# The cached pages of a decode step as a four-stage pipeline in a ring of 1 MB units

## The chip, the cores and the metric

The kernel runs on one core of a Trainium2 chip. The metric is device time in microseconds (us) of one execution, as the median of three runs. Engines are named as in the profile: PE is TensorE (matmuls; PEld its weight loads), DVE is VectorE, ACT is ScalarE, POOL is GpSimd, SP is SyncE, which here mostly issues DMAs. A name with a q (SPq) is an engine's sequencer.

## The reference, cut to what matters

The program is one step of a two-layer hybrid decoder, in float32, for a prompt of 1024 tokens and for 8 samples of 4 new tokens each. A layer has a combined input projection, a gated delta rule recurrence (4 heads) beside differential attention (8 key heads of 64, 4 value heads of 128), an output projection, cross attention and a gated MLP. For the samples, differential attention also looks at 4096 past tokens, which lie in pages of 128 tokens and are found through a table:

```python
past_k = cache_k[l][page_table].reshape(Bs, past_len, 2 * DIFF_H, DIFF_DH)
past_v = cache_v[l][page_table].reshape(Bs, past_len, DIFF_H, DIFF_DV)
...
s = jnp.einsum('bqhd,bkhd->bhqk', qi, k).astype(jnp.float32) * scale
p = jax.nn.softmax(s, axis=-1).reshape(B, H, 2, qb, Lk)
a = p[:, :, 0] - lam * p[:, :, 1]
return jnp.einsum('bhqk,bkhe->bqhe', a.astype(v.dtype), v)
```

Per layer and sample these are 32 key pages and 32 value pages of 256 KB, so 128 MB of keys and values in each of the two layers.

## The kernel before, in words

The program is written as generators that record instructions and yield a cost. `interleave` always continues the generator that has used the least of its budget. In each layer two run together: the main stream (`rest`: projections, recurrence, attention of the prompt; then `post`: output projection, cross attention, MLP for the first half of the tokens) with a budget of 520 + 2 x 450, and the page stream (`dec`, then `dec_end`) with 152. The second half of `post` follows alone. A scheduler then sets the order of each engine's queue from the recorded order, from priorities, and from its own model of when operands are ready; on the chip every engine works through its queue in that order and waits where an operand is not there. `prio(n)` moves what is recorded in it ahead by n places in the scheduler's eyes.

`dec` goes through the samples one after the other. For keys it has 8 steps S per sample, each of four pages. A half step loads two pages into a tile `kn` (`pages`, ring of 3 of 512 KB) and transposes them on DVE into half of a tile `T` (L653). When both are there, 16 matmuls (L657, in `prio(20000)`) give scores in the PSUM tile `sc`, which after four steps are reduced to a maximum and copied to `p` (two buffers). After step 7 comes the exponential on ACT, then 8 transposes of `p` on PE (L672, also in `prio`) with copies to `pT`. Then 8 steps of values: four pages are loaded into `vn`, and four matmuls (L681, in `prio`) add to the PSUM tile `po`. `T` and `vn` share one ring of four buffers of 1 MB, tag `pg`. So a key load is recorded right ahead of its transpose, and a value load right ahead of its matmuls.

`pages` reads the page numbers into SP's registers and issues one DMA of 256 KB for each page on SP. It keeps the page loads in their order, and behind the weight fetch recorded last (`anchor`; `issue_after` sets an order in a queue and no wait). The weights are fetched on SP too (`fetch`, L315), into a ring `raw`; ACT casts a tile to `whi` (L332) and POOL makes the rest `wlo` (L333); three matmuls a product use them (L353 to L355). SP takes fetches and page loads from one queue, in order.

Of the kernel before, what the change touches and what calls it, by code (L numbers as in the profile page):

```python
# [9 lines left out]
F32 = mybir.dt.float32  # L10
# [9 lines left out]
P = 128  # L20
# [3 lines left out]
NB = 8  # L24
# [159 lines left out]
def build(tc, a, out, depth=2):  # L184
# [20 lines left out]
    v_, s_, g_, t_ = nc.vector, nc.scalar, nc.gpsimd, nc.tensor  # L205
# [380 lines left out]
    for l in range(depth):  # L586
# [38 lines left out]
        def dec_open():  # L625
# [5 lines left out]
            qs = dk.tile([P, 2048], F32, name="qs", tag="pg", bufs=4)[0:32, 0:512]  # L631

        def dec():
            mlq = dk.tile([P, 16, 32], BF16, name="mlq")
# [5 lines left out]
            yield 0.1  # L640
            for b in range(NB):
                lq = dk.tile([P, 16, 32], F32, name="lq", tag="lq", bufs=1)
                g_.tensor_tensor(lq.rearrange("p a (m q) -> p a m q", q=4), bcast(Q0[:, :, 4 * b:4 * b + 4], 2, 8), mlq.rearrange("p a (m q) -> p a m q", q=4), op=ALU.mult)
                p = dk.tile([P, 1024], F32, name="p", tag="p", bufs=2)
                m2 = dk.tile([P, 2], F32, name="m2", tag="m2", bufs=2)
                for S in range(8):
                    if S % 4 == 0:
                        sc = psB((P, 512))
                    T = dk.tile([P, 4, 16, 32], F32, name="T", tag="pg", bufs=4)
                    for hf in range(2):  # L650
                        kn = dk.tile([P, 2, 512], F32, name="kn", tag="kn", bufs=3)
                        pages(b * NPG + S * 4 + 2 * hf, 2, lambda i: kn[:, i, :], lambda r: ckl[bass.ds(r, 1)].rearrange("o t h d -> (o t) (h d)"))
                        v_.transpose(T[:, 2 * hf:2 * hf + 2].rearrange("p s j b -> p (s j b)"), kn.rearrange("p s d -> p (s d)"))  # L653
                    with prio(int(XP[3])):
                      for j in range(4):
                        for c in range(4):
                            t_.matmul(sc[32 * c:32 * c + 32, (S % 4) * P:(S % 4 + 1) * P], lq[:, 4 * c + j, :], T[:, :, 4 * c + j, :], start=(j == 0), stop=(j == 3))  # L657
                    if S % 4 == 3:
                        v_.tensor_reduce(m2[:, S // 4:S // 4 + 1], sc, axis=AX.X, op=ALU.max)
                        evac(p[:, (S // 4) * 512:(S // 4) * 512 + 512], sc)  # L660
                    yield 1.2
# [1439 lines left out]
```

## Time and profile before

| What | Value |
|---|---|
| median of three runs | 4379.74 us (4379.24 to 4381.07) |
| the profiled execution | 4376.1 us, its span 4374.0 us |
| PE, PEld busy | 3896.6 us (89%), 3308.6 us (76%) |
| DVE, ACT, POOL busy | 2542.2, 1483.0, 1580.3 us |
| mean granted PE clock | 0.943 |
| bytes read from and written to HBM | 589.71 MB, 79.25 MB |

The span is the time from the first to the last instruction in the trace; the execution's own time is 2.1 us more. Busy time counts an engine's work without its waits. The granted clock is the share of TensorE's full 2.4 GHz that the chip granted; at each moment it is 1.0 or 0.5. Idle time of an engine that is not the bottleneck costs nothing.

### The profile page before, as it was taken

The numbers are of one execution on the slowest core, as the hardware profiler recorded it, in microseconds if no ns is written. First come the engines' busy times: TensorE is split into PE (matmuls) and PEld (weight loads), VectorE is DVE, ScalarE is ACT, GpSimd is POOL, SyncE is SP. The second block draws the span as 40 slices with busy tenths as digits, with TensorE's granted clock in tenths as the row PEclk, the third lists the DMA queues.
The fourth block names the chain that finished last, engine by engine and source line by source line (L and its number), as shares of the span: only waits on it lengthen the run. The fifth ranks groups of instructions, "written<-read, shape, count | busy, mean of one in ns | idle before, by whom it ended". The sixth has DMA issues, their size and how long they took to land. (4 is left out here: it accounts for less than half of the span.)

```text
span 4374.0 us, 77980 instructions
## 1 busy us (share of the span) xinstructions
PE 3896.6 (89%) x28558; PEld 3308.6 (76%) x28558; DVE 2542.2 (58%) x4573; ACT 1483.0 (34%) x3086; POOL 1580.3 (36%) x1402
## 2 busy tenths in 40 slices
PE   6999988888888998899989998888789899989999
PEld 5888856676666678899989886666666666878999
DVE  7536747655555654566576275667366555456555
ACT  4333443433222224333233253334242222342222
POOL 6542422132333343444446142311323233424442
PEclk8999979998999999999999998899889999999999
DMA  5657677567687764322246467654758876532222
GB/s 171 180 142 185 190 178 205 127 199 192 165 206 189 203 162 126 98 74 83 84 118 192 122 186 203 195 146 126 205 155 217 215 200 160 158 97 74 84 84 75
DMA packets 684806, 674.11 MB, mean 154 GB/s; under 512 B 70397, under 2 KB 501448, under 8 KB 684424
## 3 DMA queue, kind: packets, MB, share of 16 engines
q1 hardware_dynamic: 637909, 638.99, 53.7%
q10 hardware_dynamic: 44851, 25.81, 1.9%
q8 instruction: 226, 3.70, 0.4%
q0 software_dynamic: 1664, 4.33, 0.3%
q14 instruction: 156, 1.28, 0.1%
HBM read 589.71 MB, written 79.25 MB: 153 GB/s over the span
## 5 line engine op out<-in xcount | busy, mean ns | idle before, releaser
L333 POOL TENSOR_TENSOR wlo<-raw,whi 128x1024 fp32r<-128x1024 f32 (+1 forms) x472 | 929.5, 1977 | 1291.6 <-ACT whi L332 1228.9
L353 PE MATMUL psA<-ph,whi 128*128 128x272 f32 (+2 forms) x2784 | 884.7, 320 | 37.3 <-ACT ph L389 17.7
L354 PE MATMUL psA<-pl,whi 128*128 128x272 f32 (+2 forms) x2784 | 882.5, 318 | 12.4 <-POOL pl L392 12.4
L355 PE MATMUL psA<-ph,wlo 128*128 128x272 f32 (+2 forms) x2784 | 881.4, 318 | 0.0
L332 ACT CAST whi<-raw 128x1024 fp32r<-128x1024 f32 (+1 forms) x472 | 407.4, 873 | 1027.6 <-PE psA L354 565.4
L353 PEld LDWEIGHTS psA<-ph,whi 128*128 128x128 f32 x2784 | 533.8, 193 | 89.5 <-ACT ph L389 21.1
L354 PEld LDWEIGHTS psA<-pl,whi 128*128 128x128 f32 x2784 | 535.7, 193 | 53.8 <-POOL pl L392 14.2
L355 PEld LDWEIGHTS psA<-ph,wlo 128*128 128x128 f32 x2784 | 534.4, 192 | 41.0 <-issue 11.6
L653 DVE STREAM_TRANSPOSE T<-kn 128x1024 f32<-128x1024 f32 x256 | 315.8, 1237 | 181.1 <-DMA kn<-in_cache_k_dram 170.9
L353 PE MATMUL psA<-ah,whi 128*128 128x272 f32 (+2 forms) x948 | 313.0, 346 | 24.8 <-DVE fcv L2006 14.8
L2020 DVE TENSOR_TENSOR x<-x,psA 128x272 f32<-128x272 f32 (+2 forms) x474 | 233.8, 516 | 167.7 <-PE psA L355 164.3
L354 PE MATMUL psA<-al,whi 128*128 128x272 f32 (+2 forms) x948 | 307.5, 337 | 7.9 <-DVE al L309 7.7
L355 PE MATMUL psA<-ah,wlo 128*128 128x272 f32 (+2 forms) x948 | 295.1, 335 | 9.9 <-POOL wlo L333 9.9
L353 PE MATMUL psA<-hi,hh 128*128 128x256 f32 (+3 forms) x864 | 252.8, 294 | 36.0 <-DVE cxn L744 28.7
L681 PE MATMUL psC<-vn,pT 128*32 128x512 f32 x1024 | 154.4, 680 | 133.3 <-DMA vn<-in_cache_v_dram 117.2
L353 PE MATMUL psA<-hh,whi 128*128 128x352 f32 x768 | 255.4, 333 | 5.5 <-ACT whi L332 5.5
L355 PE MATMUL psA<-hi,hl 128*128 128x256 f32 (+3 forms) x864 | 251.0, 291 | 6.1 <-POOL hl L392 3.5
L355 PE MATMUL psA<-hh,wlo 128*128 128x352 f32 x768 | 253.7, 331 | 1.0 <-POOL wlo L333 1.0
L354 PE MATMUL psA<-hl,whi 128*128 128x352 f32 x768 | 254.4, 331 | 0.0
L354 PE MATMUL psA<-lo,hh 128*128 128x256 f32 (+3 forms) x864 | 251.5, 292 | 0.0
L353 PEld LDWEIGHTS psA<-ah,whi 128*128 128x128 f32 x948 | 184.0, 197 | 76.1 <-DVE fcv L2006 21.2
L309 DVE TENSOR_TENSOR al<-fcv,ah 128x272 fp32r<-128x272 f32 (+2 forms) x134 | 200.8, 1502 | 63.9 <-ACT ah L308 63.4
(553 smaller groups left out, 7970.3 us busy)
## 6 DMA issues: line engine op xcount, KB each, us to landing
kn<-in_cache_k_dram SPq DMA_DIRECT2D x512, 256.0 KB
vn<-in_cache_v_dram SPq DMA_DIRECT2D x512, 256.0 KB
raw<-in_w_gate_dram SPq DMA_DIRECT2D x88, 512.0 KB
raw<-in_w_up_dram SPq DMA_DIRECT2D x88, 512.0 KB
raw<-in_w_down_dram SPq DMA_DIRECT2D x88, 512.0 KB
qksc<-ctt ACTq DMA_DIRECT2D x128, 128.0 KB
raw<-in_w_in_dram SPq DMA_DIRECT2D x128, 128.0 KB
raw<-in_w_out_dram SPq DMA_DIRECT2D x32, 512.0 KB
```

Source lines behind the costliest of these rows:

```text
L309: eng.tensor_tensor(lo, src, hi.bitcast(F32), op=ALU.subtract)
L332: s_.copy(hi, raw)
L333: g_.tensor_tensor(lo, raw, hi.bitcast(F32), op=ALU.subtract)
L353: t_.matmul(ps, ahi, bhi, start=(i == 0), stop=False)
L354: t_.matmul(ps, ahi, blo, start=False, stop=False)
L355: t_.matmul(ps, alo, bhi, start=False, stop=(i == n - 1))
L653: v_.transpose(T[:, 2 * hf:2 * hf + 2].rearrange("p s j b -> p (s j b)"), kn.rearrange("p s d -> p (s d)"))
L681: t_.matmul(po[32 * i:32 * i + 32, :], pT[:, i, S, :], vn[:, i, :], start=(S == 0), stop=(S == 7))
L2020: v_.tensor_tensor(x[:, ot, cs], x[:, ot, cs], ps, op=ALU.add)
```

## The change

`dec` is written anew. Its work is cut into units of 1 MB: four key pages or four value pages, all in one ring of four buffers (tag `pg`), while `T` gets a ring of its own (tag `T`, two buffers, which also takes `qs` and a tile of `dec_end`). The list `seq` sets the order of the units: the keys of sample 0; then for each sample b the keys of sample b+1 and, behind them, the values of b. At the step of unit i four things are recorded: the load of unit i+3; for a key unit its transposes; the score matmuls of the key unit of the step before (`late`); for a value unit its matmuls. The transposes of the probabilities of sample b-1 are recorded after key unit 2 of sample b. `p` has one buffer.

The matmuls are no longer in `prio`. `Tracked` notes the last instruction that the main stream recorded on DVE and PE, and `behind` queues the page stream's instructions on that engine behind it. The line of every DVE and PE instruction is thereby that of the wrapper, L217. The budget is 153 for 152.

```diff
-                    T = dk.tile([P, 4, 16, 32], F32, name="T", tag="pg", bufs=4)
-                    for hf in range(2):
-                        kn = dk.tile([P, 2, 512], F32, name="kn", tag="kn", bufs=3)
-                        pages(b * NPG + S * 4 + 2 * hf, 2, lambda i: kn[:, i, :], lambda r: ckl[bass.ds(r, 1)].rearrange("o t h d -> (o t) (h d)"))
-                        v_.transpose(T[:, 2 * hf:2 * hf + 2].rearrange("p s j b -> p (s j b)"), kn.rearrange("p s d -> p (s d)"))
-                    with prio(int(XP[3])):
...
+            seq = [("k", 0, S) for S in range(8)]
             for b in range(NB):
+                if b + 1 < NB:
+                    seq += [("k", b + 1, S) for S in range(8)]
+                seq += [("v", b, S) for S in range(8)]
...
+            def load(i):
+                if i >= len(seq):
+                    return
+                kind, b, S = seq[i]
+                t = dk.tile([P, 4, 512], F32, name=kind + "n", tag="pg", bufs=4)
+                pgs[i] = t
...
+            for i, (kind, b, S) in enumerate(seq):
+                load(i + 3)
+                t = pgs.pop(i)
+                if kind == "k":
+                    T = dk.tile([P, 4, 16, 32], F32, name="T", tag="T", bufs=2)
+                    with behind(v_):
+                        for hf in range(2):
+                            v_.transpose(T[:, 2 * hf:2 * hf + 2].rearrange("p s j b -> p (s j b)"), t[:, 2 * hf:2 * hf + 2].rearrange("p s d -> p (s d)"))
+                if late is not None:
+                    yield 0.6
+                    products(*late)
+                    late = None
+                if kind == "k":
+                    late = (b, S, T)
+                    if b == 1 and S == 0:
+                        queries(1)
+                    if b and S == 2:
+                        yield 0.5
+                        pT = transposed(b - 1)
+                    yield 0.6
+                    continue
...
+                with behind(t_):
+                    for j in range(4):
+                        t_.matmul(po[32 * j:32 * j + 32, :], pT[:, j, S, :], t[:, j, :], start=(S == 0), stop=(S == 7))
+                yield 1.0
...
-        for _ in interleave((chain(rest(), scaled(post(0, HALF, False), PSC)), 520.0 + PSC * 450), (chain(ahead(dec(), TUNE[6]), ahead(dec_end(), TUNE[8])), 152.0)):
+        for _ in interleave((chain(rest(), scaled(post(0, HALF, False), PSC)), 520.0 + PSC * 450), (aside(chain(dec(), dec_end())), 153.0)):
```

**First place: values of the fifth sample of layer 0, beside the MLP's weights.** In SP's queue before, raw_15190 and raw_15196 are the fetches of one gate and one up tile; each value unit is four DMAs, of which one is shown.

```order
L315 DMA raw_15190<-in_w_gate_dram 128x8x128
L315 DMA raw_15196<-in_w_up_dram 128x8x128
...
L622 DMA vn_15241<-in_cache_v_dram 32x4x512
...
L622 DMA vn_15312<-in_cache_v_dram 32x4x512
...
L315 DMA raw_15358<-in_w_gate_dram 128x8x128
```

On PE before, whi_14804 is the up tile of the group of fetches before these, and whi_15192 the cast of raw_15190.

```order
L353 MATMUL psA_15073<-ph1_13834,whi_14804 128x512
L354 MATMUL psA_15073<-pl1_13835,whi_14804 128x512
L681 MATMUL psC_14868<-vn_15241,pT_14831 32x512 x4
L355 MATMUL psA_15073<-ph1_13834,wlo_14805 128x512
...
L353 MATMUL psA_15210<-ph0_11888,whi_15192 128x512
L681 MATMUL psC_14868<-vn_15312,pT_14831 32x512 x4
```

In SP's queue of the change, raw_15920 and raw_15926 are the fetches of a gate and an up tile.

```order
L354 DMA raw_15920<-in_w_gate_dram 128x8x128
...
L661 DMA vn_15604<-in_cache_v_dram 32x4x512
...
L354 DMA raw_15926<-in_w_up_dram 128x8x128
...
L661 DMA vn_15713<-in_cache_v_dram 32x4x512
...
L661 DMA vn_15803<-in_cache_v_dram 32x4x512
```

On PE of the change, whi_15922 is the cast of raw_15920 and whi_15928 that of raw_15926.

```order
L217 MATMUL psC_15684<-vn_15604,pT_15071 32x512 x4
L217 MATMUL psA_15940<-ph0_12048,whi_15922 128x512
...
L217 MATMUL psC_15684<-vn_15713,pT_15071 32x512 x4
L217 MATMUL psA_16017<-ph0_12048,whi_15928 128x512
...
L217 MATMUL psC_15684<-vn_15803,pT_15071 32x512 x4
```

Before, vn_15241 stood behind an up fetch on SP and was used ahead of the whole gate group that was fetched ahead of it; now vn_15713 stands behind an up fetch and is used a gate group later, right ahead of that up tile's matmuls.

**Second place: the first keys of the next sample, same layer.** On DVE before, kn_15480 holds the first half unit; the product psA_15287 is made with the up tile whose fetch is raw_15196.

```order
L653 STREAM_TRANSPOSE T_15479<-kn_15480 128x1024
L2006 TENSOR_TENSOR fcv_15209<-fcv_15209,psA_15287 128x512
L653 STREAM_TRANSPOSE T_15479<-kn_15503 128x1024
L309 TENSOR_TENSOR al_15203<-fcv_15209,ah_15202 128x512
L684 TENSOR_TENSOR om_15463<-psC_14868,c_hm_1853 128x512
```

SP's queue before goes on, behind raw_15358 of the first place, with its up tile, two down tiles, one more value unit and then these keys.

```order
L315 DMA raw_15364<-in_w_up_dram 128x8x128
L315 DMA raw_15373<-in_w_down_dram 128x1024
L315 DMA raw_15379<-in_w_down_dram 128x1024
...
L622 DMA vn_15393<-in_cache_v_dram 32x4x512
...
L622 DMA kn_15480<-in_cache_k_dram 128x512
```

On DVE of the change the same place has these rows; psA_14864 is made with the up tile whose fetch is raw_14768.

```order
L217 TENSOR_TENSOR al_14775<-fcv_14562,ah_14774 128x256
L217 SCALAR_TENSOR_TENSOR fcv_14784<-fraw_14782,pvf0_127,fcv_14784 128x512 x2
L217 STREAM_TRANSPOSE T_14861<-kn_14473 128x1024 x2
L217 STREAM_TRANSPOSE T_14931<-kn_14614 128x1024 x2
L217 TENSOR_TENSOR fcv_14784<-fcv_14784,psA_14864 128x512
```

In SP's queue of the change kn_14473 is a whole unit of four DMAs.

```order
L354 DMA raw_14762<-in_w_gate_dram 128x8x128
L354 DMA raw_14768<-in_w_up_dram 128x8x128
...
L661 DMA vn_14385<-in_cache_v_dram 32x4x512
...
L661 DMA kn_14473<-in_cache_k_dram 128x512
...
L354 DMA raw_14996<-in_w_gate_dram 128x8x128
```

The transpose stands at the same place of the MLP in both; the load that feeds it has moved up SP's queue, past four fetches and two value units.

**Third place: values of the first sample of layer 0, on PE of the change.** The eight value units of the sample are vn_4880, vn_5083, vn_5349, vn_5573, vn_5900, vn_6056, vn_6204 and vn_6350; between the second (row 2247) and the third (row 2536) stand 288 other rows.

```order
L217 MATMUL psC_5734<-vn_5349,pT_4402 32x512 x4
L217 MATMUL psG_6102<-kt_6037 128x128 x4
L217 MATMUL psC_5734<-vn_5573,pT_4402 32x512 x4
L217 MATMUL psC_5734<-vn_5900,pT_4402 32x512 x4
L217 MATMUL psC_5734<-vn_6056,pT_4402 32x512 x4
L217 MATMUL psA_6799<-c_ident_63,cst_6683 27x128
...
L217 MATMUL psA_6958<-hl0_102,whi_6746 128x352
L217 MATMUL psC_5734<-vn_6204,pT_4402 32x512 x4
```

Four units stand together here, and vn_6204, whose buffer is that of vn_5349, follows 27 rows behind it.

## Rows read from the trace of the kernel before

**Rows 1.** The page's span and its part 1, busy time by engine.

```profile
span 4374.0 us, 77980 instructions
...
PE 3896.6 (89%) x28558; PEld 3308.6 (76%) x28558; DVE 2542.2 (58%) x4573; ACT 1483.0 (34%) x3086; POOL 1580.3 (36%) x1402
```

**Rows 2.** Windows: start:end, length, busy by engine, granted clock, DMA share, GB/s.

```profile
180.00:1560.00 1380.00, 1211.61 (x8860) 961.65 (x8859) 801.96 (x1406) 460.81 (x1045) 441.43 (x441) 0.93 0.70 183
1560.00:2280.00 720.00, 662.29 (x4937) 624.47 (x4935) 442.20 (x810) 246.58 (x418) 304.54 (x226) 0.96 0.33 101
2280.00:3680.00 1400.00, 1234.79 (x9079) 989.06 (x9078) 805.57 (x1462) 475.00 (x1092) 447.51 (x456) 0.93 0.68 181
3680.00:4374.00 694.00, 648.34 (x4854) 611.29 (x4852) 384.05 (x707) 222.32 (x365) 267.55 (x187) 0.98 0.31 95
```

**Rows 3.** Groups of PE: busy us, mean ns | idle before, who ended it.

```profile
L681 PE MATMUL psC<-vn,pT 128*32 128x512 f32 x1024 | 154.4, 680 | 133.3 <-DMA vn<-in_cache_v_dram 117.2 <-issue 7.7 <-ACT pT L673 2.9
L657 PE MATMUL psB<-T,lq 128*32 128x128 f32 x4096 | 146.4, 288 | 47.8 <-DVE T L653 37.0 <-POOL lq L643 2.9 <-DVE mx L1397 2.3
...
L672 PE MATMUL psC<-c_ident,p 128*128 128x128 f32 x128 | 19.8, 278 | 4.7 <-ACT p L665 4.3 <-ACT pT L673 0.4
```

**Rows 4.** Waits of PE: us in total, times, longest us.

```profile
PE psA L353 <- DVE cxn L744: 28.7, 6, 16.7
PE psA L353 <- ACT whi L332: 22.0, 6, 7.4
...
PE psA L355 <- POOL wlo L333: 10.9, 17, 1.4
```

**Rows 5.** Group of DVE: the transposes of keys.

```profile
L653 DVE STREAM_TRANSPOSE T<-kn 128x1024 f32<-128x1024 f32 x256 | 315.8, 1237 | 181.1 <-DMA kn<-in_cache_k_dram 170.9 <-issue 9.3
```

**Rows 6.** Timeline of SP, 1140 to 1200: start, us, what, count.

```profile
1141.33 7.77 SPq L622 DMA_DIRECT2D vn<-in_cache_v_dram  x8
1150.06 0.40 SPq L315 DMA_DIRECT2D raw<-in_w_gate_dram  x1
1151.29 0.72 SPq L315 DMA_DIRECT2D raw<-in_w_up_dram  x1
1153.96 9.41 SPq L622 DMA_DIRECT2D vn<-in_cache_v_dram  x8
...
1186.07 12.04 SPq L622 DMA_DIRECT2D kn<-in_cache_k_dram  x12
```

**Rows 7.** Timeline of DVE, 1185 to 1200; in brackets idle before it.

```profile
1191.24 1.25 DVE L653 STREAM_TRANSPOSE T<-kn 128x1024 f32<-128x1024 f32 x1 [4.19 <-DMA kn<-in_cache_k_dram]
```

**Rows 8.** Timeline of PE, 1160 to 1182.

```profile
1167.95 1.93 PE L681 MATMUL psC<-vn,pT 128*32 128x512 f32 x8 [2.74 <-DMA vn<-in_cache_v_dram]
...
1172.03 0.39 PE L353 MATMUL psA<-ph,whi 128*128 128x512 f32 x1
...
1179.54 0.39 PE L353 MATMUL psA<-ph,whi 128*128 128x512 f32 x1
```

**Rows 9.** Waits of SP's queue.

```profile
SPq L315 <- POOL wlo L333: 926.8, 258, 17.7
```

**Rows 10.** Windows late in the page stream of each layer.

```profile
1200.00:1400.00 200.00, 178.86 (x1184) 129.76 (x1183) 112.35 (x117) 49.06 (x64) 63.14 (x42) 0.96 0.78 201
1400.00:1560.00 160.00, 142.06 (x856) 101.38 (x855) 78.03 (x80) 37.15 (x48) 51.44 (x33) 0.98 0.81 198
...
3400.00:3680.00 280.00, 254.05 (x1556) 182.30 (x1556) 150.30 (x155) 68.71 (x88) 92.91 (x62) 0.98 0.80 204
```

**Rows 11.** Windows of 25 us, full and half empty.

```profile
1525.00:1550.00 25.00, 21.09 (x93) 13.79 (x86) 5.22 (x8) 2.10 (x2) 4.80 (x2) 0.86 1.09 218
1350.00:1375.00 25.00, 25.00 (x221) 19.82 (x220) 14.74 (x15) 11.05 (x15) 11.76 (x8) 1.00 0.45 149
```

**Rows 12.** Line L681: shortest, median and longest ns, first and last start.

```profile
L681 PE MATMUL psC<-vn,pT x1024: 589/617/1062, 324.5 to 3676.9; 128*32 128x512 f32 x171
```

**Rows 13.** Timeline of ACT, 1140 to 1170.

```profile
1160.21 1.05 ACT L332 CAST whi<-raw 128x1024 fp32r<-128x1024 f32 x1 [21.33 <-DMA raw<-in_w_gate_dram]
```

More of the change, by code (lines that the diff above doesn't have):

```diff
@@ L204, in build, with __init__, __getattr__, call @@
     QD = {'0': nc.gpsimd, '1': nc.scalar, '2': nc.sync}[XP[0]]
-    v_, s_, g_, t_ = nc.vector, nc.scalar, nc.gpsimd, nc.tensor
+    beside = [False]
+    class Tracked:
+        def __init__(self, eng):
+            self.eng, self.last = eng, None
+        def __getattr__(self, name):
+            f = getattr(self.eng, name)
+            def call(*args, **kw):
+                r = f(*args, **kw)
+                if not beside[0]:
+                    self.last = r
+                return r
+            return call
+    v_, s_, g_, t_ = Tracked(nc.vector), nc.scalar, nc.gpsimd, Tracked(nc.tensor)
+    def behind(*engs):
+        st_ = ExitStack()
+        for e in engs:
+            st_.enter_context(tc.issue_after(e.last.ins))
+        return st_
+    def aside(g):
+        while True:
+            beside[0] = True
+            try:
+                c = next(g)
+            except StopIteration:
+                return
+            finally:
+                beside[0] = False
+            yield c
     es = ExitStack()
@@ new lines, in dec, with products @@
+            cur = {}
+            def products(b, S, T):
+                if S == 3:
+                    cur["p"] = dk.tile([P, 1024], F32, name="p", tag="p", bufs=1)
+                    cur["m2"] = dk.tile([P, 2], F32, name="m2", tag="m2", bufs=2)
+                if S % 4 == 0:
+                    cur["sc"] = psB((P, 512))
+                sc, p, m2 = cur["sc"], cur.get("p"), cur.get("m2")
+                lq = lqs[b]
+                with behind(t_):
+                    for j in range(4):
@@ L675, in dec @@
-                po = psC()
-                for S in range(8):
-                    vn = dk.tile([P, 4, 512], F32, name="vn", tag="pg", bufs=4)
-                    pages(b * NPG + S * 4, 4, lambda i: vn[32 * i:32 * i + 32, :, :], lambda r: cvl[bass.ds(r, 1)].rearrange("o (i b) h e -> (o b) i (h e)", i=4))
-                    with prio(int(XP[3])):
-                      for i in range(4):
-                        t_.matmul(po[32 * i:32 * i + 32, :], pT[:, i, S, :], vn[:, i, :], start=(S == 0), stop=(S == 7))
-                    yield 0.9
@@ L683, in dec @@
[L683 to L686 removed]
+                return pT
+            late = None
+            queries(0)
+            for i in range(3):
+                load(i)
@@ L1484, in dec_end @@
         def dec_end():
-            df = Carve(dk.tile([P, 2048], F32, name="T", tag="pg", bufs=4))
+            df = Carve(dk.tile([P, 2048], F32, name="T", tag="T", bufs=2))
             nmask = cload(df, "nmask", rows=32)
```

69 lines of the change are left out of this document (42 added, 27 removed).

## The prediction

> **What bounds the kernel now.** I read the page first [rows 1]: over a span of 4374.0 us TensorE (PE) is busy for 3896.6 us (89%), no other engine for more than 58%. So the time is PE's work, what the granted clock takes from it, and the holes in it. Then the windows, cut where the page stream (the reading of the samples' cached keys and values) starts and ends in each layer [rows 2]. The two stretches with it last 1380 and 1400 us. PE is idle there for 168.4 and 165.2 us, 333.6 in all, at a mean granted clock of 0.93; the stretches without it stand at 0.96 and 0.98. DMA is busy for 0.70 and 0.68 of a stretch with the stream and for about a third of one without.
>
> Then the groups of PE, to see which matmuls the holes stand ahead of [rows 3]: 133.3 us before the stream's value products (L681), 47.8 before its score products (L657), 4.7 before its transposes (L672). That is 185.8 us, over half of 333.6, ahead of work that itself takes 320.6 us. The same rows name the releaser: the landing of the value pages for 117.2 us, and for the scores the transposes on VectorE (DVE). DVE in turn stands for 181.1 us before these transposes, 170.9 of it on key pages [rows 5].
>
> One case of each shows why. Keys: SP, whose queue issues the loads, starts the first one at 1186.07 [rows 6], and the transpose at 1191.24 has waited 4.19 us for it [rows 7]: a half unit takes 5.2 us to land and is wanted at once. Values: vn_15241 is the first of the two units whose loads start at 1153.96 [rows 6]; PE takes it at 1167.95 after 2.74 us of nothing [rows 8]. PE works in order, so every matmul behind waits as well, those of the prompt included, whose data had long been there. The scheduler was told (offset 20000) to put the stream's matmuls as early as it believed them ready; the pages come later than it believed.
>
> **What the change does, and the sum.** It is made against the profiled execution, 4376.1 us; the median of the runs is 3.6 above that.
>
> *Work.* None is added: the same 256 transposes on DVE, the same matmuls, the same 1024 page DMAs of 256 KB. SP reads 256 instead of 384 groups of page numbers; it spends 926.8 us waiting for weight buffers to come free [rows 9], so this is worth nothing, and would be if it cost something.
>
> *Lead of the loads.* This is the whole change. In the order shown first, for the fifth sample in layer 0, vn_15713 is queued right behind the fetch raw_15926 and used right before the first matmul of that fetch's weights. In the trace the up fetch of that place, raw_15196, starts at 1151.29 [rows 6], and its first matmul runs at 1179.54 [rows 8]: some 28 us, where the load of vn_15241 had 14 and was 2.74 late. For keys (second place of the order) both kernels transpose the next sample's first unit just before DVE takes the product with one up fetch's weights. Before, that unit was queued behind three value units and four more fetches after this one; now it is queued behind a single value unit, so by the same rows some 30 us ahead. The products of a key unit also come one step later than its transposes, so PE no longer waits for DVE directly.
>
> *Waits that stay.* Twice the cover is thin. (a) In the first layer four value units are used in one clump behind a long stretch of other matmuls (third place of the order): the ring of four is full till then, the next load starts only there, its use is some 25 rows later, and it is late by about a landing: 5.2 us for half a unit [rows 6, 7]. I keep 6 us. (b) The late stretches: 1200 to 1560 and 3400 to 3680 have DMA shares of 0.78, 0.81 and 0.80 [rows 10], 510 us of full DMA in 640 us, while PE is busy for 575. Without any hole in PE the share would be 510/575 = 0.89, and slices of 25 us already stand as high as 1.09, with 0.45 between them [rows 11]. Evening them out over 3 MB of ring does not get all of it. Of the 65.0 us that PE is idle there I keep half, 32. So of 185.8 us there go 185.8 - 6 - 32 = **148** (bounds: all 185.8; or half, see the first rival).
>
> *Other work freed.* DVE no longer holds the prompt's work behind a transpose. The nearest row is PE's 28.7 us of waits for cxn, which DVE makes [rows 4]; they may have nothing to do with it, or all. I take half, **14** (0 to 28.7).
>
> *Clock.* A matmul of the value group takes 589 ns at the shortest and 1062 at the longest [rows 12], about the ratio of the two levels, 2.4 and 1.2 GHz. With fewer holes the stream's stretches should come nearer to the 0.96 to 0.98 of the others. That most of the gap of 0.03 to 0.05 stays is likely, since the attention and recurrence there make holes of their own: I take 0.02 of 2780 us = **56** (0, to 0.05 x 2780 = 139).
>
> *Given back.* The waits that aren't the stream's are 333.6 - 185.8 = 147.8 us. When PE comes sooner, it meets other engines that are not ready. In the last stretch, without pages, 45.7 of 694 us are idle, 6.6%. 6.6% of the 2562 us that would be left is 169, so **+21** (0 to 60, by the 8.0% of 1560 to 2280).
>
> *At nothing.* One buffer for p instead of two: the next sample's first scores are written to it after unit 3, and the transposes that free it stand behind unit 2; what covers that is a step of other work, of which 256 share 2780 us. If it failed, the scores would wait for a copy of one tile, 16 times. Tiles moved between rings, and a budget of 153 for 152, move no work.
>
> Sum: -148 - 14 - 56 + 21 = -197, so 4179 in a profiled execution, **4183** against the median.
>
> The Trainium skill (TensorE: Matmul & The Clock Gate, Terms) values the low clock at the throttled time times one half. A mean of 0.93 over 2780 us is 389 us at half rate, so 195 us, and the sum by it would be 4376 - 148 - 14 - 195 + 21 = 4040, if the stream had caused it all. The ratio in [rows 12] agrees with the half; the 0.96 and 0.98 of the stretches without the stream [rows 2] say that part of it would stay.
>
> **New waits.** Each load now waits for the buffer used four units before, where the rings of before held 1.5 units of keys and four of T and vn; behind it on SP wait the weight fetches. That buffer is mostly free about a step before. DVE gets its two transposes of a key unit back to back, 2 x 1.237 us [rows 5], as it did when both halves had landed.
>
> **Rivals.**
> 1. *The bandwidth is the wait.* The bursts at a share over 1 would then last as long as before, wherever the loads are queued. For it: [rows 11]. Against: the 0.45 between, and a mean of 0.70. Half of the 185.8 stays, the clock gains 0.01 (28): 4376 - 93 - 28 = 4255, against the median 4259.
> 2. *The clock follows to 0.98.* For it: the last stretch. Against: 0.96 between the layers, where no page is read. 4376 - 148 - 14 - 139 + 21 = 4096, 4100 against the median.
> 3. *Slower: weights come late behind pages.* Pages are queued further ahead, on the queue of the fetches. Its place: ScalarE's cast of a gate tile. For it: a fetch issued at 1150.06 behind eight page loads [rows 6] is cast at 1160.21, after 21.33 us of waiting [rows 13]. Against: the weights are used 12 us later, at 1172.03 [rows 8], and PE's waits for them are only 22.0 and 10.9 us in the whole span [rows 4]. It decides once the 256 units cost PE more than 197/256 = 0.77 us each; at 1 us the time is 4376 - 197 + 256 = 4435, 4439 against the median. The Trainium skill (DMA: Bandwidth & Descriptors, Queues, rings and completion order) says that each DMA engine takes a ring's descriptors in order, which is this mechanism; the 10 us from issue to cast agree.
> 4. *No change.* The holes only move to the next wait of the prompt's chain: 4380. For it: ACT, DVE and POOL run chains with PE in the attention. Against: 6.6% in the last stretch.
>
> **How the numbers follow.** My forecast 0.56, with its own range of 4140 to 4230 (the 38 us that stay gone or doubled, or the clock off by 0.01, which is 28, and a little of both); rival 1 0.20; rival 2 0.12; rival 3 0.08; rival 4 0.04. A measurement of this kernel tells about 0.2% from no change. Faster by more than that: 0.56 + 0.20 + 0.12 = 0.88; within it 0.04; slower 0.08. The range of 4095 to 4300 takes in the forecast and rivals 1 and 2 with the bounds between them; outside are rivals 3 and 4 and the far end of 2, some 0.17.
>
> **What would show it.** In the profile after: idle before the value, score and transpose matmuls together about 38 us instead of 185.8; DVE's idle before its transposes under 40 instead of 181.1; mean clock of the two stretches near 0.95; and about 90 us less in each layer. If the DMA share of the late stretches comes to 0.9 and the stream's waits stay near 90, it is rival 1; if the waits of ACT's casts for fetches reach PE as waits for whi and wlo, rival 3. The prediction is wrong if the stream's waits go and the span does not follow by about as much: then they were not what bounded it.

## The result and the profile after

The changed kernel takes **4242.23 us** (median of 4 runs, 4234.21 to 4243.3) against 4380.4 beside it: ratio 0.968 (95% interval 0.966 to 0.969), 138 us less. The forecast was 4183. The sign held, and so did the range of 4095 to 4300, but 4242 lies above the forecast's own range of 4140 to 4230. Of the 197 us that it summed, 63 did not come.

The page of the changed kernel, its first lines, as in [rows 1]:

```profile
span 4240.4 us, 77767 instructions
...
PE 3860.1 (91%) x28558; PEld 3287.4 (78%) x28558; DVE 2516.0 (59%) x4574; ACT 1486.3 (35%) x3085; POOL 1575.9 (37%) x1402
```

The span falls by 133.6 us. Of that PE's busy time gives 3896.6 - 3860.1 = 36.5 and its idle time (span less busy) 477.4 - 380.3 = 97.1.

The groups of PE and DVE that answer to [rows 3] and [rows 5]; every line is now L217, the wrapper's:

```profile
L217 PE MATMUL psB<-T,lq 128*32 128x128 f32 x4096 | 155.0, 288 | 12.6 <-DVE T L217 9.6 <-POOL lq L728 3.0
...
L217 PE MATMUL psC<-vn,pT 128*32 128x512 f32 x1024 | 139.7, 624 | 3.0 <-DMA vn<-in_cache_v_dram 3.0
...
L217 PE MATMUL psC<-c_ident,p 128*128 128x128 f32 x128 | 19.5, 275 | 0.5 <-ACT pT L738 0.5
...
L217 DVE STREAM_TRANSPOSE T<-kn 128x1024 f32<-128x1024 f32 x256 | 301.3, 1217 | 41.0 <-PE psB L217 37.1 <-DMA kn<-in_cache_k_dram 3.8 <-issue 0.2
```

The stream's waits on PE are 12.6 + 3.0 + 0.5 = 16.1 us, where they were 185.8. DVE waits 3.8 us for key pages, where it was 170.9. So idle time ahead of all other matmuls went the other way: from 477.4 - 185.8 = 291.6 to 380.3 - 16.1 = 364.2, **72.6 us more**.

The windows, cut where the stream starts and ends as in [rows 2], then three late ones as in [rows 10] (columns: length, PE, PEld, DVE, ACT, POOL busy, granted clock, DMA share, GB/s):

```profile
180.00:1510.00 1330.00, 1203.58 (x8885) 964.23 (x8885) 784.67 (x1409) 463.85 (x1048) 439.04 (x445) 0.93 0.73 190
1510.00:2200.00 690.00, 638.35 (x4802) 602.78 (x4800) 418.73 (x756) 239.13 (x390) 285.94 (x201) 0.97 0.33 99
2200.00:3560.00 1360.00, 1244.23 (x9276) 998.28 (x9278) 827.99 (x1540) 490.66 (x1126) 471.68 (x482) 0.95 0.72 190
3560.00:4240.00 680.00, 636.61 (x4775) 602.32 (x4775) 376.13 (x680) 214.98 (x356) 260.70 (x183) 0.97 0.31 95
```

```profile
1200.00:1400.00 200.00, 193.21 (x1285) 141.89 (x1287) 117.20 (x126) 52.12 (x68) 70.61 (x48) 0.98 0.87 226
1400.00:1510.00 110.00, 106.02 (x529) 72.23 (x521) 47.46 (x52) 28.67 (x37) 38.50 (x26) 0.97 0.87 194
3300.00:3560.00 260.00, 250.58 (x1479) 175.54 (x1477) 139.22 (x167) 70.85 (x91) 92.40 (x61) 0.99 0.83 201
```

By this cut some time without the stream counts as part of the second stretch. From the start of the first page load to that of the last value matmul the stretches last 1375.9 and 1409.2 us before, 1327.8 and 1321.9 after: 48 and 87 us less. Between them lie 713 us in both kernels, and behind the second 697.1 and 704.5. So the gain lies in the stretches. Their clock is 0.93 and 0.95, where it was 0.93 in both.

In the late windows PE is idle for only 20.2 of 570 us (65.0 of 640 in [rows 10]), at a DMA share (of the time of the core's 16 DMA engines) of 0.83 to 0.87. The last window reaches 24 us past the stream's end; up to there, in 3300 to 3536, the share is 0.89.

The waits of PE after (us in all, times, longest), and three of the same waits before:

```profile
PE psA L217 <- DVE cxn L217: 29.6, 8, 16.7
PE psA L217 <- DVE fcv L217: 27.0, 26, 4.0
PE psA L217 <- ACT ph L428: 25.4, 11, 8.5
PE psA L217 <- ACT whi L371: 25.0, 7, 11.2
PE psA L217 <- POOL pl L431: 18.5, 10, 2.9
...
PE psA L217 <- ACT phx L1864: 13.7, 2, 9.2
...
PE psG L217 <- DMA S<-in_state_gdn_dram: 10.5, 6, 3.9
PE psA L217 <- POOL wlo L372: 9.9, 16, 1.4
```

```profile
PE psA L353 <- ACT ph L389: 17.7, 8, 4.9
PE psA L353 <- DVE fcv L2006: 14.8, 22, 3.3
PE psG L1285 <- DMA S<-in_state_gdn_dram: 1.7, 2, 1.5
```

What was given back is spread: fcv 12 us more, phx 12, S 9, ph 8, pl 6, and many small ones. Summed by the engine that ended the wait, over all matmuls but the stream's, ACT rises from 79.6 to 120.3 us, DVE from 109.8 to 131.1, DMA from 36.1 to 43.4, POOL from 57.4 to 60.7.

How far ahead a unit is loaded can be read by counting: from the issue of the first of its DMAs on SP to the first transpose or matmul that uses it. The 38th value unit, shown in [rows 6] and [rows 8] with 14 us between, is after the change:

```profile
1188.28 1.83 SPq L661 DMA_DIRECT2D vn<-in_cache_v_dram  x4
```

```profile
1215.36 1.93 PE L217 MATMUL psC<-vn,pT 128*32 128x512 f32 x16
```

27 us ahead, with no wait. Over the 128 units of a kind the median from issue to use is 4.9 us (keys) and 9.5 (values) before, 35.4 and 27.6 after.

### The profile page after: what moved, and what is told of

Read it like the earlier page. It is cut to its first block, busy times and chain, and to the rows that moved or that the text cites. A ratio compares the mean times of both kernels' runs of the same rounds, so it can differ in the third digit from the quotient of the medians.

```text
span 4240.4 us, 77767 instructions
## 1 busy us (share of the span) xinstructions
PE 3860.1 (91%) x28558; PEld 3287.4 (78%) x28558; DVE 2516.0 (59%) x4574; ACT 1486.3 (35%) x3085; POOL 1575.9 (37%) x1402
## 5 line engine op out<-in xcount | busy, mean ns | idle before, releaser
L217 PE MATMUL psA<-ph,whi 128*128 128x272 f32 (+2 forms) x2784 | 887.6, 321 | 50.4 <-ACT ph L428 25.4
L217 PE MATMUL psA<-pl,whi 128*128 128x272 f32 (+2 forms) x2784 | 880.4, 317 | 22.8 <-POOL pl L431 18.5
L217 PE MATMUL psA<-ph,wlo 128*128 128x272 f32 (+2 forms) x2784 | 877.7, 316 | 0.1
L217 PEld LDWEIGHTS psA<-ph,whi 128*128 128x128 f32 x2784 | 532.7, 192 | 126.4 <-ACT ph L428 29.3
L217 PEld LDWEIGHTS psA<-pl,whi 128*128 128x128 f32 x2784 | 535.1, 192 | 56.7 <-POOL pl L431 21.1
L217 PEld LDWEIGHTS psA<-ph,wlo 128*128 128x128 f32 x2784 | 533.9, 192 | 31.1 <-issue 1.9
L217 DVE TENSOR_TENSOR x<-x,psA 128x272 f32<-128x272 f32 (+2 forms) x590 | 285.0, 499 | 337.3 <-PE psA L217 302.9
L217 PE MATMUL psA<-ah,whi 128*128 128x272 f32 (+2 forms) x948 | 312.9, 346 | 40.8 <-DVE fcv L217 27.0
L217 DVE STREAM_TRANSPOSE T<-kn 128x1024 f32<-128x1024 f32 x256 | 301.3, 1217 | 41.0 <-PE psB L217 37.1
L217 PE MATMUL psA<-al,whi 128*128 128x272 f32 (+2 forms) x948 | 311.7, 337 | 11.4 <-DVE al L217 11.2
L217 PE MATMUL psA<-ah,wlo 128*128 128x272 f32 (+2 forms) x948 | 302.9, 335 | 9.3 <-POOL wlo L372 9.3
L217 PE MATMUL psA<-hi,hh 128*128 128x256 f32 (+3 forms) x864 | 254.6, 296 | 45.2 <-DVE cxn L217 29.6
L217 PE MATMUL psA<-hh,whi 128*128 128x352 f32 x768 | 254.0, 331 | 4.2 <-ACT whi L371 4.2
L217 PE MATMUL psA<-hi,hl 128*128 128x256 f32 (+3 forms) x864 | 249.7, 290 | 5.8 <-POOL hl L431 3.5
L217 PE MATMUL psA<-hh,wlo 128*128 128x352 f32 x768 | 253.0, 330 | 0.6 <-POOL wlo L372 0.6
L217 PEld LDWEIGHTS psA<-ah,whi 128*128 128x128 f32 x948 | 183.9, 197 | 87.7 <-DVE fcv L217 35.1
L217 PE MATMUL psA<-hl,whi 128*128 128x352 f32 x768 | 251.7, 328 | 0.0
L217 PE MATMUL psA<-lo,hh 128*128 128x256 f32 (+3 forms) x864 | 249.8, 290 | 0.1
L217 DVE TENSOR_TENSOR al<-fcv,ah 128x272 fp32r<-128x272 f32 (+2 forms) x134 | 192.1, 1437 | 76.4 <-ACT ah L347 75.8
L217 DVE TENSOR_SCALAR fcv<-fraw,pvf 128x512 f32<-128x512 f32 x88 | 126.4, 1436 | 143.3 <-ACT fraw L2080 143.2
```

Of the source, the lines that this page charges most:

```text
L217: r = f(*args, **kw)
```

## The experiments

All in one table. The ratio is to the kernel before, run on the same chip, with its 95% interval. The kernels ran in four groups, beside which the kernel before took 4380.4, 4378.57, 4368.3 and 4374.94 us, so two variants are compared by their ratios. "Issue to use" is the median just described, for keys and for values. PE's busy and idle time, the idle time ahead of the stream's matmuls, and DVE's ahead of the page transposes are those of the profiled execution, in us, which lies up to 15 us from the median of its kernel. "Behind" means queued by `behind`, after the main stream's last instruction on that engine.

| Kernel | Ratio | Issue to use | PE busy | PE idle | stream | DVE idle |
|---|---|---|---|---|---|---|
| before | 1 | 4.9, 9.5 | 3896.6 | 477.4 | 185.8 | 181.1 |
| before, matmuls behind | 0.994 (0.993 to 0.996) | 5.1, 18.8 | 3912.3 | 439.1 | 13.1 | 222.0 |
| before, transposes behind | 0.987 (0.986 to 0.989) | 14.0, 11.8 | 3867.7 | 450.4 | 153.6 | 41.8 |
| before, both behind | 0.975 (0.971 to 0.979) | 14.0, 17.9 | 3866.8 | 392.0 | 60.3 | 45.4 |
| **changed** | 0.968 (0.966 to 0.969) | 35.4, 27.6 | 3860.1 | 380.3 | 16.1 | 41.0 |
| changed, no lead | 0.970 (0.968 to 0.971) | 24.1, 20.4 | 3869.4 | 378.7 | 49.6 | 43.3 |
| changed, lead of 1 | 0.971 (0.970 to 0.973) | 29.1, 24.4 | 3863.8 | 385.8 | 29.7 | 40.8 |
| changed, matmuls with priority | 0.993 (0.991 to 0.994) | 43.7, 10.1 | 3882.2 | 478.8 | 194.7 | 2.4 |
| changed, transposes free | 0.975 (0.971 to 0.979) | 34.3, 29.5 | 3888.1 | 382.5 | 9.9 | 170.5 |
| changed, old order of units | 0.980 (0.977 to 0.984) | 30.8, 34.5 | 3885.5 | 397.9 | 34.2 | 8.0 |
| changed, scores not late | 0.974 (0.972 to 0.976) | 37.1, 26.0 | 3879.3 | 384.1 | 20.6 | 22.9 |
| changed, three T | 0.966 (0.964 to 0.967) | 26.1, 19.3 | 3874.0 | 366.9 | 30.9 | 25.6 |
| changed, budget 170 | 0.978 (0.976 to 0.980) | 32.6, 25.6 | 3877.1 | 398.9 | 15.5 | 36.3 |
| changed, no page traffic | 0.951 (0.947 to 0.954) | | 3847.8 | 311.3 | 8.9 | 42.2 |

**Is it the lead of the loads?** That was the prediction's reason. The rivals: the dropped priority, or the order of the units. First, the load at the unit's own step:

```diff
-            for i in range(3):
+            for i in range(0):
                 load(i)
...
-                load(i + 3)
+                load(i + 0)
```

> The changed kernel with the load of a unit recorded at the unit's own step, right ahead of its use, instead of three units before; order of the units, matmuls without priority and everything else stay. If the lead of the loads is what removed the waits, they come back: idle time ahead of the stream's matmuls 150 us or more (16 in the changed kernel, 186 before) and 4370 to 4450 us. If dropping the priority or the new order of the units did it, the time stays within 30 us of the changed kernel's 4242 and the waits stay under 60 us.

And with one step (`range(1)`, `load(i + 1)`):

> The changed kernel with each load recorded one unit ahead of its use instead of three. A unit's step is some 2780/256 = 11 us of the page stream. Before, a value unit whose load had started 14 us ahead was 2.7 us late, and a half key unit took 5 us to land: with 11 us added most units should be there. Lead as the cause, and one step nearly enough: stream's waits 20 to 60 us, 4245 to 4290 us. If the ring's depth evens out bursts of bandwidth (slices at a DMA share over 1 beside slices at 0.45), one unit is too little: waits of 80 us or more and over 4300 us.

Measured: 4248.54 and 4251.58 us, ratios 0.970 and 0.971, against 0.968. The groups of the kernel without a lead:

```profile
L217 PE MATMUL psC<-vn,pT 128*32 128x512 f32 x1024 | 140.3, 625 | 28.0 <-DMA vn<-in_cache_v_dram 22.4 <-DMA kn<-in_cache_k_dram 3.7 <-issue 1.9
...
L217 DVE STREAM_TRANSPOSE T<-kn 128x1024 f32<-128x1024 f32 x256 | 301.6, 1218 | 43.3 <-PE psB L217 36.1 <-DMA kn<-in_cache_k_dram 7.2
```

The theory as put falls. A load that is recorded right ahead of its use is still issued 24 or 20 us ahead of it. That fits the order on SP: the load stands behind the latest weight fetch, and one such fetch ran some 28 us ahead of its first matmul [rows 6, 8]; no run shows this link by itself.

The three units of lead add 11 and 7 us. Much of the lead is spent on SP, which waits ahead of page loads until a transpose or a product has freed a tile. These are its waits in the changed kernel, then without a lead:

```profile
SPq L661 <- DVE T L217: 196.7, 44, 20.7
SPq L661 <- PE psC L217: 109.6, 48, 10.7
```

```profile
SPq L661 <- DVE T L217: 41.4, 19, 6.7
SPq L661 <- PE psC L217: 34.6, 18, 11.1
```

The lead removes 34 us of the stream's waits, but the idle time ahead of all other matmuls is 35 us longer with it (364.2 for 329.1), and PE's idle time in all is the same. It brings 0.2%, at the edge of what can be told. One step of lead stays in the range that was given for lead as the cause, but so does no lead at all, so that run decides nothing.

**Is it the priority?** The priority is replaced by `behind` in the kernel before, at all three places (one is shown), with loads, rings and order untouched; and the other way round, it is put back in the changed kernel. No run drops the priority without `behind` in its place, so the two are not told apart.

```diff
-                    with prio(int(XP[3])):
+                    with behind(t_):
                       for j in range(4):
```

> The kernel before with its page stream's matmuls queued behind the main stream's last recorded matmul in place of the priority of 20000; loads, rings and order of the units stay as before. If the priority was the cause (matmuls stood ahead of work that was ready), most of the gain appears: under 4300 us, stream's waits under 80 us. If the lead of the loads is the cause, little of it does: 4350 to 4450 us, waits of 130 us or more.

```diff
-                with behind(t_):
+                with prio(int(XP[3])):
```

> The changed kernel with the priority of 20000 back on the stream's matmuls in place of their being queued behind the main stream's; loads still three units ahead. If the lead is the cause, it stays near the changed kernel: 4225 to 4275 us, stream's waits under 50 us. If the priority is the cause, most of the loss returns: over 4320 us and waits over 110 us.

Measured: 4352.61 (0.994) and 4348.19 us (0.993). Each by itself looks as if the priority were worth little, or nearly all. The profile shows why. The kernel before with only its matmuls behind; groups, two waits of PE, and a piece of DVE's timeline:

```profile
L217 PE MATMUL psC<-vn,pT 128*32 128x512 f32 x1024 | 139.3, 625 | 5.6 <-DMA vn<-in_cache_v_dram 5.5
...
L217 DVE STREAM_TRANSPOSE T<-kn 128x1024 f32<-128x1024 f32 x256 | 315.0, 1236 | 222.0 <-DMA kn<-in_cache_k_dram 218.4 <-PE psB L217 2.3
```

```profile
PE psA L217 <- DVE fcv L217: 46.0, 26, 8.3
...
PE psA L217 <- DVE al L217: 20.9, 9, 5.6
```

```profile
1208.54 1.25 DVE L217 STREAM_TRANSPOSE T<-kn 128x1024 f32<-128x1024 f32 x1 [2.90 <-DMA kn<-in_cache_k_dram]
1209.71 0.65 DVE L217 TENSOR_TENSOR al<-fcv,ah 128x512 fp32r<-128x512 f32 x1
```

The waits for values are gone (133.3 to 5.6 us). But DVE now waits 218.4 us for key pages, and the prompt's work stands behind the transpose, as `al` does in the last line. PE's waits for DVE ahead of matmuls that aren't the stream's, summed over the whole trace, are 226 us, where they were 110 before. The changed kernel with its priority back has the opposite: DVE waits for no page, and PE waits for values.

```profile
L217 PE MATMUL psC<-vn,pT 128*32 128x512 f32 x1024 | 160.1, 692 | 167.0 <-DMA vn<-in_cache_v_dram 147.8 <-issue 7.7 <-DMA in<-gdsc 5.3
```

Its value units are loaded three units ahead too, and are used 10.1 us after issue, where `behind` gives 27.6: with the priority the use moves up to the load. So there are two queues in which uses stand too early, and a new theory: what counts is where the uses stand on both. Three runs test it.

**Both queues, and DVE's alone, in the kernel before.** The first has the edit above as well as this one, the second this one alone:

```diff
-                        v_.transpose(T[:, 2 * hf:2 * hf + 2]...
+                        with behind(v_):
+                            v_.transpose(T[:, 2 * hf:2 * hf + 2]...
```

> The kernel before with both of its page stream's queues put behind the main stream: matmuls in place of the priority, and transposes on VectorE. Loads, rings, units and their order stay as before. Theory A: the waits come from where the uses stand in the queues, and from nothing else; with both moved the load of a key half unit should start 15 us or more ahead of its use (4.9 us before), VectorE's waits for keys fall from 181 us to under 60, and the time to 4230 to 4275 us. Theory B: the new rings and the order of the units are needed as well (a ring of three half units is too short for keys): waits for keys stay over 120 us and the time over 4310 us.

> The kernel before with only its transposes queued behind the main stream on VectorE; the matmuls keep the priority of 20000. With the two runs that moved the matmuls alone (ratio 0.994 to before) and both (0.975) it completes the four. Theory A (either queue alone passes the wait on to the other): VectorE's waits for keys fall under 80 us, PE's waits ahead of the stream's matmuls stay over 130 us, 4310 to 4380 us. Rival (VectorE's place is what matters, the matmuls follow): under 4290 us and PE's stream waits under 90 us.

Measured: 4261.45 (0.975) and 4320.9 us (0.987). The groups of both behind, then of the transposes alone:

```profile
L217 PE MATMUL psB<-T,lq 128*32 128x128 f32 x4096 | 145.8, 282 | 36.0 <-DVE T L217 32.8 <-ACT p L700 2.2 <-DVE zba L217 0.8
L217 PE MATMUL psC<-vn,pT 128*32 128x512 f32 x1024 | 140.5, 630 | 16.2 <-DMA vn<-in_cache_v_dram 8.6 <-ACT pT L713 7.5
```

```profile
L217 PE MATMUL psC<-vn,pT 128*32 128x512 f32 x1024 | 146.4, 669 | 110.7 <-DMA vn<-in_cache_v_dram 92.2 <-ACT pT L713 15.1 <-issue 2.6
...
L217 DVE STREAM_TRANSPOSE T<-kn 128x1024 f32<-128x1024 f32 x256 | 304.1, 1221 | 41.8 <-DMA kn<-in_cache_k_dram 41.7
```

Both times fall as Theory A has it. Matmuls alone bring 0.6%, transposes alone 1.3%, together 2.5%, more than their sum of 1.8%. With no new ring, no new order and no lead the old kernel has 2.5 of the 3.2% of the change. That either queue alone passes its waits on to the other is not seen for the transposes: with them alone moved, PE's waits ahead of the stream fell from 185.8 to 153.6 us. With both, the first load of a key unit is issued 14.0 us ahead; counted by half units, as the expectation was, it is 10.3 and not 15, with 45 us of waits left.

**The transposes free again in the changed kernel.**

```diff
-                    with behind(v_):
+                    with nullcontext():
```

> The changed kernel with its transposes no longer queued behind the main stream's last instruction on VectorE; matmuls stay behind, loads stay three units ahead in the ring of 1 MB units. Theory A (place of the uses): VectorE waits for key pages again, 100 us or more, its waits pass to the prompt's matmuls, and the time comes to 4300 to 4370 us. Theory B (lead of the loads and the ring): loads three units ahead cover this too, waits for keys under 40 us, 4235 to 4260 us.

4265.51 us (0.975): between the two theories, 35 us under the range of the first and 5.5 over that of the second, on a chip where the kernel before took 4368.3.

```profile
L217 DVE STREAM_TRANSPOSE T<-kn 128x1024 f32<-128x1024 f32 x256 | 306.1, 1224 | 170.5 <-PE psB L217 93.0 <-DMA kn<-in_cache_k_dram 76.8
```

The ring and the lead do cover part: 76.8 us of waits for keys instead of 170.9; another 93.0 us are waits for a free T. Against the changed kernel the place of the transposes is worth 0.7%, where it was 2.0% in the kernel before with its matmuls behind (0.9944 to 0.9748).

**The order of the units.**

```diff
-            seq = [("k", 0, S) for S in range(8)]
-            for b in range(NB):
-                if b + 1 < NB:
-                    seq += [("k", b + 1, S) for S in range(8)]
-                seq += [("v", b, S) for S in range(8)]
+            seq = [(kind, b, S) for b in range(NB) for kind in "kv" for S in range(8)]
...
-                    if b and S == 2:
-                        yield 0.5
-                        pT = transposed(b - 1)
```

> The changed kernel with the units of a sample in the old order: eight of keys, then eight of values, with the transposes of the probabilities right ahead of the values. Ring, lead of three units, places in the queues and late score products stay. If the order matters only as a chain of exponential, transposes and copies that PE waits for at each of 16 samples (some 2 to 4 us each), it costs 20 to 60 us: 4260 to 4300 us, with waits ahead of the transposes of p or of the first value products. If the order is worth nothing, it is within 10 us of 4242.

4287.48 us (0.980), 1.3% over the changed kernel. Its waits of PE:

```profile
PE psA L217 <- ACT whi L371: 48.3, 16, 8.6
...
PE psC L217 <- ACT p L717: 21.7, 8, 6.8
```

The chain is there: 21.7 us, eight times, for the exponential, ahead of the transposes of p. The wait for weights that ACT casts has nearly doubled too (25.0 to 48.3). PE's idle time in all is 17.6 us more and its busy time 25.4, the latter at a lower clock (0.944 for 0.948).

**The late score products.**

```diff
-                if late is not None:
...
-                    late = (b, S, T)
+                    yield 0.6
+                    products(b, S, T)
```

> The changed kernel with the score products of a key unit at the same step as its transposes, not one step later. If the extra step is what lets PE find T ready, PE's waits for T rise from 9.6 us to 30 us or more (32.8 in the kernel before with both queues moved, which has no such step), and the time to 4255 to 4280. If it is worth nothing: within 8 us of 4242.

4265.18 us (0.974), in the range expected, but not for its reason: the wait for T is 17.1 us, not 30. Idle time rises by 3.8 us and busy time by 19.2. The step is worth 0.7%, most of it in busy time, of which the low clock takes 170.2 us for 151.2 (the next section says how this is counted); why it does stays open.

**What the traffic still costs.** All units after the fourth of a layer work on the four tiles that were loaded first, so the kernel leaves out the traffic and its values are not the cache's.

```diff
-                t = dk.tile([P, 4, 512], F32, name=kind + "n", tag="pg", bufs=4)
-                pgs[i] = t
+                t = pgs[i] = fixed[i % 4] if fixed[i % 4] is not None else dk.tile(...)
+                if fixed[i % 4] is not None:
+                    return
+                fixed[i % 4] = t
```

> The changed kernel without its page traffic: only the first four units of each layer are loaded, and all later units work on these four tiles, so the values read are not the cache's; transposes and matmuls all stay. It shows what the traffic still costs after the change. The stream's own waits are 16 us there. If the 78.5 us of other waits that came instead of the stream's are the prompt's own chains, the time falls by 10 to 40 us, to 4200 to 4232. If they are transfers that share the bandwidth with the pages (the recurrence's states, the queries, the weights), it falls by 60 us or more, under 4180.

4158.97 us: 0.951 against 0.968, 1.7% or 74 us of 4380. The windows of the two stretches:

```profile
180.00:1510.00 1330.00, 1235.14 (x9106) 996.82 (x9106) 809.85 (x1465) 484.66 (x1076) 460.52 (x457) 0.95 0.33 95
...
2200.00:3560.00 1360.00, 1279.46 (x9439) 1028.82 (x9438) 839.41 (x1520) 507.48 (x1121) 482.65 (x472) 0.96 0.33 96
```

At a DMA share of 0.33 the waits that aren't the stream's are 311.3 - 8.9 = 302.4 us, where the changed kernel has 364.2 and the one before 291.6. So 62 of the 72.6 us given back go with the traffic in this pair. This isn't a fixed price: the kernel without a lead, with all its traffic, has 329.1.

**A better version?** Three T for four pages, and an earlier stream:

```diff
-                    T = dk.tile([P, 4, 16, 32], F32, name="T", tag="T", bufs=2)
+                    T = dk.tile([P, 4, 16, 32], F32, name="T", tag="T", bufs=3)
...
-                t = dk.tile([P, 4, 512], F32, name=kind + "n", tag="pg", bufs=4)
+                t = dk.tile([P, 4, 512], F32, name=kind + "n", tag="pg", bufs=3)
...
-                load(i + 3)
+                load(i + 2)
```

> The changed kernel with three buffers of T instead of two, three of the page ring instead of four, and loads two units ahead. In the changed kernel VectorE waits 37.1 us for score products to free a T, six times, most of it in the clumps at the start of the layers; the place in the rings is to go there from the pages, since a load recorded one unit ahead did as well as three. If this wait holds the prompt's work on VectorE: 10 to 35 us less than 4242. If PE has other work meanwhile: within 8 us of it, with the wait gone all the same.

```diff
-(aside(chain(dec(), dec_end())), 153.0)
+(aside(chain(dec(), dec_end())), 170.0)
```

> The changed kernel with a budget of 170 for the page stream instead of 153, so that its units come earlier in the layer and its end earlier too. In the changed kernel the DMA share is 0.87 between 1200 and 1510 us and 0.72 over the stretch, and leaving the traffic out took 74 us off. If the crowding of the late part is what the traffic costs, the late share falls under 0.80 and the time by 10 to 40 us. If it costs wherever it is, the time stays within 8 us or rises, since the early part of the layer has less other work to hide units behind.

Three T: 4227.26 us (4225.7 to 4242.74), ratio 0.966 (0.964 to 0.967) against 0.968 (0.966 to 0.969): the lowest of all with the whole computation, but the intervals overlap, so whether it is better stays open. Its profiled execution is the slowest of its five (4242.74). DVE's wait for a free T halves, where it was expected to go, and PE's for values rises:

```profile
L217 PE MATMUL psC<-vn,pT 128*32 128x512 f32 x1024 | 140.0, 624 | 17.9 <-DMA vn<-in_cache_v_dram 17.8
...
L217 DVE STREAM_TRANSPOSE T<-kn 128x1024 f32<-128x1024 f32 x256 | 300.5, 1216 | 25.6 <-PE psB L217 19.5 <-DMA kn<-in_cache_k_dram 6.1
```

Budget 170: 4282.53 us (0.978), 40 us more and 1.1% by the ratios. Its windows:

```profile
1200.00:1510.00 310.00, 298.07 (x1760) 215.21 (x1759) 171.37 (x209) 89.85 (x115) 113.83 (x75) 0.99 0.78 189
...
3300.00:3560.00 260.00, 245.28 (x1372) 172.96 (x1371) 134.16 (x174) 72.14 (x92) 89.77 (x62) 0.97 0.77 185
```

By these windows the late share falls to 0.78 and 0.77, but only because the stream ends inside them. Its last value matmul starts at 1432.9 and 3493.9 us, where it was 1500.6 and 3535.9. Up to there the share is higher than in the changed kernel (0.88 and 0.89):

```profile
1200.00:1433.00 233.00, 223.02 (x1416) 156.89 (x1414) 122.50 (x132) 62.41 (x81) 81.22 (x54) 0.99 0.93 221
3300.00:3494.00 194.00, 184.96 (x1102) 126.79 (x1100) 90.02 (x103) 50.40 (x64) 60.98 (x42) 0.97 0.93 217
```

So the earlier stream did not relieve its end, it crowded it more, and the time rose. The run speaks neither for nor against crowding as what the traffic costs. Idle time ahead of matmuls other than the stream's is 398.9 - 15.5 = 383.4 us, 19 more than in the changed kernel.

## Why the prediction was right, and where it was not

| Term | Forecast | Measured in the profiled executions |
|---|---|---|
| the stream's waits on PE | -148 | 185.8 to 16.1: -169.7 |
| other idle time of PE (freed -14, given back +21) | +7 | 291.6 to 364.2: +72.6 |
| clock, as busy time of PE | -56 | 3896.6 to 3860.1: -36.5 |
| sum | -197 | -133.6 |

*What bounds the kernel.* Right in the direction: uses stood ahead of their pages, PE and DVE waited in order, and with the waits gone the time fell. By the prediction's own sign, that the span follows "by about as much", it held in part: 169.7 us of the stream's waits went, and PE's idle time fell by 97.1, the span by 133.6.

*"Lead of the loads. This is the whole change."* This step failed. The time from issue to use did rise to about 30 us, as worked out, and the runs divide it. The places of the uses alone, in the old rings, take it from 4.9 and 9.5 us to 14.0 and 17.9; ring, order and late products to 24.1 and 20.4; the loads recorded three units ahead to 35.4 and 27.6. In time the first part brings 2.5 of the 3.2%, and the last 0.2%. The prediction had named the priority as what put the matmuls early, and gave its removal no term of its own. Of the transposes it saw the wait, but took their place to be the same in both kernels, from the one transpose of the second place, and credited the load. Ring, order, late products and lead together bring the other 0.7%. Taken out of the changed kernel singly, order and late products cost 1.3 and 0.7%, so the parts don't add up.

*Waits that stay.* 38 forecast, 16.1 measured. The clump was to cost 6 us: in all of the value units one wait of 3.0 stands, at the eighth. The late stretches were to keep 32 of 65.0 us of idle time: in the late windows above all idle time of PE together is 20.2. The share did come to 0.87 there, and to 0.89 up to the stream's end in the second layer, as worked out.

*At nothing.* The single `p` held: ACT's copies to it wait for DVE's maxima (84.6 us, 79.1 before), and none for the transposes on PE that free it. The rings moved "at nothing" did not: with two T, DVE waits 37.1 us for score products to free one. This is why DVE's idle time is 41.0 and not under 40, nearly all of it no longer for pages.

*New waits.* The buffer of a unit was to be "mostly free about a step before". SP waits for it 92 times all the same, 306.3 us in all, by the rows shown with the lead.

*Given back.* The term that was mis-sized most: -14 + 21 against +72.6. The cxn wait that was to fall by half stayed (28.7 to 29.6). The 6.6% were taken from a stretch without pages, which is the likeliest error: without page traffic 302.4 us remain, near the 291.6 of before; with it 364.2. Traffic isn't all of it, for with the same traffic and 34 us more of the stream's waits only 329.1 us remain (no lead). It seems that before, the stream's own waits hid part of what the others wait for. That is argued from these sums; no run separates bandwidth from the order in SP's queue.

*Clock.* 0.943 to 0.948 by the page, 0.93 to 0.93 and 0.93 to 0.95 by stretch, and not 0.02 in both. At each moment the traces' clock records show 1.0 or 0.5. Time at 0.5, counted by half, adds up to 248.2 us before and 220.1 after. Of these, 192.6 and 151.2 us fall within PE's busy time, the rest within its idle time. Busy time less that part is 3704.0 and 3708.9 us, so the fall of busy time is all clock, as far as the modelled ends of the matmuls tell. The Trainium skill (TensorE: Matmul & The Clock Gate, Terms) values throttled time at one half. The traces agree: busy time less the half of its throttled time lies between 3697.5 and 3716.1 us in all fourteen kernels, where busy time itself runs from 3847.8 to 3912.3. What failed is the size, 56 for 36.5: 97 of 477 us of idle time are gone, and 28 of 248 us returned. Even without page traffic the clock is only 0.952.

*Signs.* The stream's waits are under the 38 us given, and DVE's idle time is 41.0 for "under 40". "About 90 us less in each layer" came as 48 and 87 us in the stretches, and the clock of "near 0.95" in the second alone.

*Rivals.* 1 (bandwidth): falls as put, for the stream's waits are 16 and not about 90; its 4259 is nearer to 4242 than the forecast, but by another way, since traffic does cost, at other matmuls. That the result lies in the range owes something to this rival, and so to luck. 2 (clock to 0.98): falls. 3 (weights late): whi and wlo 25.0 and 9.9 us, where they were 22.0 and 10.9; it falls here, but the old order in the new ring has it in part, at 48.3 (ACT's casts wait 49.6 us for up tiles there, 9.6 in the changed kernel). 4 (no change): falls as a whole, and is right for 73 us.

## What to carry to other kernels

Before loading earlier, measure on the chip how long it is from the issue of a load to its use, on every engine that uses it; if it is short although the load is recorded early, the use has been placed too early, and moving the use is the cheaper change. Moving it on one engine alone can pass the wait on: with only the matmuls moved, DVE's waits for pages rose from 170.9 to 218.4 us. The two moves brought 0.6% and 1.3% alone, 2.5% together. And do not count a removed wait as time won: look where else the engine then waits, in a stretch with the same traffic and not in one without.

## What was not expected of the hardware

Page traffic that nobody waits for is not free: leaving it out took the DMA share of the two stretches from 0.72 to 0.33 and 74 us off the time, 62 of them as waits of matmuls that use no page. And PE's busy time for the same 28558 matmuls varied from 3847.8 to 3912.3 us among these kernels, with the granted clock at 0.952 and 0.938; it rose where idle time was the same, as with the late products removed (19.2 us more at 3.8 us more of idle time). There the low clock takes 7.5 us more in all (227.6 for 220.1), but 19.0 more within busy time (170.2 for 151.2). So where it falls matters beside how much idle time there is; what decides that, no run here shows.
